# A Mamba-2 scan that is gated and normed in token rows, turned through DRAM

## The chip, the cores and the metric

The kernel runs on one core of a Trainium2 chip. The metric is the device time of one execution in microseconds (us), as a median over several runs.

## The reference

The kernel computes one layer of a hybrid decoder trunk over 256 tokens with 2048 features, all in float32: a token mixer with two branches (HGRN2 and Mamba-2), cross-attention into 256 memory tokens, a gated convolutional FFN, and norms between them. The change touches the Mamba-2 branch and the order around it. Cut to that:

```python
def mamba2_branch(z, xbc_raw, dt_raw, conv_w, conv_b, dt_bias, a_log, d_skip, norm_g):
    xbc = jax.nn.silu(causal_dwconv(xbc_raw, conv_w, conv_b))
    xs, bm, cm = jnp.split(xbc, [D_M2, D_M2 + M2_GROUPS * M2_DSTATE], axis=-1)
    dt = jax.nn.softplus(dt_raw + dt_bias)
    a_neg = -jnp.exp(a_log)
    y = ssd_chunk_scan(xs * dt[..., None], dt * a_neg, bm, cm)   # 8 groups of 4 heads of 64
    y = y + d_skip[:, :, None] * xs
    y = y.reshape(bsz, s, D_M2) * jax.nn.silu(z)
    yg = y.reshape(bsz, s, M2_GROUPS, D_M2 // M2_GROUPS)         # 256 features in a group
    yg = yg * lax.rsqrt(jnp.mean(yg * yg, axis=-1, keepdims=True) + M2_NORM_EPS)
    return yg.reshape(bsz, s, D_M2) * norm_g

def token_mixer(u, ...):
    hq, hf, hi, hog, mz, mxbc, mdt, g_hg, g_m2 = jnp.split(u @ w_in, idx, axis=-1)
    y_hg = hgrn2_branch(hq, hf, hi, hog, lb, hg_norm_g) @ w_branch_hg
    y_m2 = mamba2_branch(mz, mxbc, mdt, ...) @ w_branch_m2
    return (jax.nn.sigmoid(g_hg) * y_hg + jax.nn.sigmoid(g_m2) * y_m2) @ w_out
```

Group g of the Mamba-2 branch owns 256 features (two chunks of 128) of x, z and y, and 128 each of B and C. The gate and the norm work within a group, so a token's norm needs a sum over 256 features.

## The kernel before

**Matmuls.** Every weight is float32 and is cut into a high and a low part (ScalarE casts `hi`, L133; VectorE subtracts `lo`, L134), and a product is summed from three parts. Weights come in blocks of 1 MB; the list `order` fixes in which sequence SP loads them. `weights()` hands out the next block. I call the use of one block a step. There are two forms. `project` makes 128 features as rows and 256 tokens as columns ("channel rows"): 16 matmuls over 512 columns and 16 over 256 per block. `project_tok` takes four blocks and makes 2 x 128 tokens as rows and 512 features as columns ("token rows"): 24 matmuls over 512 columns per block. `raw` has 3 buffers, `hi` and `lo` have 5 halves of a block each, so casts run ahead of TensorE by up to about two blocks.

**Background.** A head's or a group's scan is a generator in the list `background`. At the start of every step each generator runs on to its next `yield`; `pause(n)` yields n times. TensorE's matmuls inside a step are pinned to that place. The other engines' instructions are put in order by a planner at build time, with its own costs; each engine then runs its queue in order, and an instruction that waits holds up what is behind it.

**The heads.** The 16 HGRN2 heads end with a turn between token rows and channel rows: `turned(y)` transposes 32x32 squares on VectorE (L503), writes the result to a DRAM tile by four transfers from POOL (L506), and reads it back in another order by one (L509). After `pause(gap)` `split_turned` scales it and cuts it into `hi` and `lo` (L515, L281, L282). `gap` is 4 steps, and 2 for the last head.

**Between.** `m2_dt` makes the steps dt and their running sums, and the Sigmoid of the first two HGRN2 gates stands at L796. The planner may put it earlier, since its input is there before the last heads.

**Mamba-2.** `m2_project(g)` makes six chunks of group g in channel rows: two of x, one of B, one of C (each with the convolution, L707 and L710) and two of z. `m2_scan(g)` then:

- takes Silu of all six chunks (L719) and builds the decays (L724 to L729); two steps later it multiplies C and B on TensorE, and turns the four 128x128 squares of x on TensorE (L747) to multiply by dt in token rows (L750);
- one step later makes the scan's product `yp` on TensorE, adds the D skip (L764), multiplies by Silu of z (L766), squares (L768) and adds the two chunks (L769);
- two steps later sums over the features by a matmul with `ones`, takes the inverse root of 128x256 values (L285, L286), and scales and cuts the result (L778, L281, L282).

`ym` holds the result for `project_tok(ym)`, the Mamba-2 branch's product. `gate()` makes the Sigmoid of 512 columns of a gate; the first two gates of this branch (`NF = 2`) come ahead of the first product, the others between the products. ScalarE holds one table of functions at a time; a function outside it takes an ACT_TABLE_LOAD.

Of the kernel before, what the change touches and what calls it, by code (L numbers as in the profile page):

```python
# [19 lines left out]
P = 128  # L20
# [44 lines left out]
def hybrid_trunk(ctx, tc, xT, memT, par, cst, msk, w_k0, w_ka, w_va, w_hg, w_hv, w_hog, w_ghg, w_bhg, w_dt,  # L65
                 w_m2, w_gm2, w_bm2, w_out, w_q, w_o, w_up, w_dn, fin_g, outT):
# [431 lines left out]
    def turned(y):  # L498

        yq = mp.tile([P, T], F32, name="yq", bufs=1)
        V.transpose(out=yq, in_=y)  # L503
        yd = dp.tile([P, T], F32, name="y_d", bufs=4)
        for b in range(P // B):
            G.dma_start(out=yd.rearrange("(n i) (b f) -> b i n f", i=B, b=P // B)[b],  # L506
                        in_=yq[b * B:(b + 1) * B, :].rearrange("i (n f) -> i n f", n=P // B))
        yc = mp.tile([P, T], F32, name="yc", bufs=2)
        G.dma_start(out=yc, in_=yd)  # L509
        return yc  # L510
# [8 lines left out]
    def hg_scan(h, kq, zz, v, sg):  # L519
# [102 lines left out]
        gap = 4 if h + 1 < HEADS else 2  # L622
        yield from pause(gap)
# [15 lines left out]
        yc = turned(y)  # L639
        yield from pause(gap)  # L640
# [17 lines left out]
    dt_tok = cp.tile([P, 2, 32], F32, name="dt_tok")  # L658
    cum_tok = cp.tile([P, 2, 32], F32, name="cum_tok")

    def m2_dt():
        ps = project(s2)
        rows = mp.tile([P, 2, T], F32, name="bb", bufs=1)
        raw, cum = rows[:, 0, :], rows[:, 1, :]
        join(mp, ps, raw)
        V.tensor_scalar(out=raw[0:32], in0=raw[0:32], scalar1=pc("dtb")[0:32], scalar2=None,
                        op0=ALU.add)
        w = mp.tile([P, T], F32, name="lf", bufs=1)
        softplus_neg_abs(raw[0:32], w[0:32])
        V.scalar_tensor_tensor(out=raw[0:32], in0=raw[0:32], scalar=0.0, in1=w[0:32],  # L670
                               op0=ALU.max, op1=ALU.add)
# [24 lines left out]

    def m2_project(g):
        sz = mp.tile([P, 6, T], F32, name="sz", bufs=2)
# [14 lines left out]
        for i in range(4, 6):  # L713
            ps = project(s2)
            join(mp, ps, sz[:, i, :])
        return sz, cb

    def m2_scan(g, sz, cb):
        S.activation(out=sz, in_=sz, func=AF.Silu)  # L719
# [24 lines left out]
        tp = pl.tile([P, 512], F32, name="lev")  # L744
        for q in range(2):
            for i in range(2):
                PE.transpose(tp[:, q * T + i * P:q * T + (i + 1) * P],  # L747
                             sz[:, i, q * P:(q + 1) * P], eye)
        xd = mp.tile([P, 2, T], F32, name="bb", bufs=1)
        V.tensor_tensor(out=xd.rearrange("p q (h c) -> p q h c", c=64),  # L750
                        in0=tp.rearrange("p (q h c) -> p q h c", q=2, c=64),
                        in1=free(dt_tok, 4 * g, [(32, 2), (1, 4), (0, 64)]), op=ALU.mult)
# [16 lines left out]
        V.tensor_tensor(out=sq[:, 0, :], in0=sq[:, 0, :], in1=sq[:, 1, :], op=ALU.add)  # L769
        yield True  # L770
        if g + 1 < GROUPS:
            yield True
        ps = pm_.tile([P, 512], F32, name="misc")
        mm(ps[:, 0:T], lhsT=ones, rhs=sq[:, 0, :], start=True, stop=True)
        r = mp.tile([P, T], F32, name="r", bufs=1)
        rsqrt(r, ps[:, 0:T], 1.0 / T, eps2_t)
        for i in range(2):
            V.scalar_tensor_tensor(out=y[:, i, :], in0=y[:, i, :], scalar=pc("m2_g", 2 * g + i),  # L778
                                   in1=r, op0=ALU.mult, op1=ALU.mult)
# [11 lines left out]
    scan = m2_scan(0, *m2_project(0))  # L791
    for c in range(4):
        o = pm[:, :, c * 512:(c + 1) * 512]
        if c < 2:
            sg = o
            S.activation(out=o, in_=o, func=AF.Sigmoid)  # L796
# [28 lines left out]
    sgs = [gate() for c in range(NF)]  # L825
    for c in range(4):
# [11 lines left out]
        if c + NF < 4:  # L838
            sgs.append(gate())
# [324 lines left out]
def _layout(inp):  # L1164
# [4 lines left out]
    z = _cols(cut(8192, 2048)).reshape(GROUPS, 2, P, 2048)  # L1169
# [20 lines left out]
    def put(name, a):  # L1190
# [35 lines left out]
        "w_m2": np.concatenate([xs, b, c, z], 1), "w_gm2": _toks(cut(16416, 2048)),  # L1226
# [24 lines left out]
```

## Time and profile before

| | |
|---|---|
| time, median of 3 runs | 2252.67 us (2252.03 to 2252.95) |
| the profiled execution | 2252.47 us, span 2250.7 us |
| TensorE busy | 2237.6 us, 99% of the span |
| VectorE busy | 1622.9 us, 72% |
| ScalarE busy | 1379.3 us, 61% |
| DMA | 441.11 MB, mean 196 GB/s |
| the heads, roughly | 160 to 560 us |
| the Mamba-2 groups 1 to 7, roughly | 700 to 980 us |

The busy share is read together with the chain of work that ended last, which says whose time set the end. A busy engine off that chain costs nothing by itself. All times on the page are from one execution.

### The profile page before, as it was taken

To read this page: it belongs to the slowest core of one execution; us is meant where nothing else is said; L and a number is where in the kernel's file an instruction comes from. 1 tells how busy PE (TensorE), PEld (TensorE's weight loads), DVE (VectorE), ACT (ScalarE), POOL (GpSimd) and SP (SyncE) were. 2 spreads that over 40 slices of the span, in tenths; PEclk is the share of its full clock that TensorE was granted. 3 is DMA by queue.
4 is the path that set the end of the run, shared out by engine and by line. 5 is a ranking of instruction groups with operands and counts; after the bars stand their busy time and mean duration, and the time that the engine had idled before them with its cause. 6 is when DMAs were issued, how large, how long until landed. Compare 5 with 4: busy or idle time off the path is not lost.

```text
span 2250.7 us, 33574 instructions
## 1 busy us (share of the span) xinstructions
PE 2237.6 (99%) x13188; PEld 1927.1 (86%) x13188; DVE 1622.9 (72%) x2602; ACT 1379.3 (61%) x2123; POOL 45.3 (2%) x89
## 2 busy tenths in 40 slices
PE   9999999999999999999999999999999999999998
PEld 8888888888888888888888888888888888888887
DVE  8858878887546677754566765677777777779787
ACT  7567677788546778764456655556555555555554
POOL 0000101101000000000000000000000000000000
PEclk9999999999999999999999999999999999999999
DMA  8655555555655555455566544476555555555554
GB/s 314 239 179 184 186 192 180 182 179 180 219 197 186 180 187 195 169 187 187 190 236 215 202 169 171 176 225 212 196 193 192 188 187 188 189 203 207 208 213 159
DMA packets 89502, 441.11 MB, mean 196 GB/s; under 512 B 25824, under 2 KB 30464, under 8 KB 40320
## 3 DMA queue, kind: packets, MB, share of 16 engines
q1 hardware_dynamic: 69600, 432.36, 54.2%
q0 software_dynamic: 2816, 4.20, 0.7%
q10 hardware_dynamic: 16928, 2.42, 0.6%
q8 instruction: 103, 1.69, 0.3%
q14 instruction: 55, 0.45, 0.1%
HBM read 430.52 MB, written 10.52 MB: 196 GB/s over the span
## 4 chain that ended last, share of the span: by engine, by line
PE 95%; ACT 2%; DVE 1%; DMA 1%; issue 1%; SPq 0%; POOL 0%; DVEq 0%; POOLq 0%; ACTq 0%
PE proj L82 86%; PE misc L82 5%; PE lev L82 4%; DVE lo L134 1%; ACT hi L133 0%; DMA yc<-y_d 0%; DMA raw<-in_w_k 0%; ACT L286 0%; DMA y_d<-yq 0%; DVE e L551 0%; ACT L285 0%; PE lev L747 0%; PE lev L816 0%; ACT y L638 0%; ACT misc L635 0%
## 5 line engine op out<-in xcount | busy, mean ns | idle before, releaser
L134 DVE TENSOR_TENSOR lo<-raw,hi 128x1024 fp32r<-128x1024 f32 x738 | 893.1, 1222 | 446.7 <-ACT hi L133 398.5
L133 ACT CAST hi<-raw 128x1024 fp32r<-128x1024 f32 x737 | 770.4, 1049 | 420.8 <-PE proj L82 391.1
L82 PE MATMUL proj<-s,hi 128*128 128x512 f32 x3696 | 873.4, 391 | 0.6 <-ACT hi L364 0.3
L82 PEld LDWEIGHTS proj<-s,hi 128*128 128x128 f32 x3696 | 685.2, 188 | 138.3 <-ACT hi L364 1.1
L82 PE MATMUL proj<-hi,s 128*128 128x512 f32 x1962 | 615.0, 390 | 0.0
L82 PEld LDWEIGHTS proj<-s,lo 128*128 128x128 f32 x3696 | 463.9, 192 | 14.2 <-DVE lo L134 2.1
L82 PE MATMUL proj<-s,lo 128*128 128x256 f32 x3696 | 472.2, 283 | 1.9 <-DVE lo L134 1.9
L82 PEld LDWEIGHTS proj<-hi,s 128*128 128x128 f32 x1962 | 368.1, 188 | 76.5 <-issue 0.3
L82 PE MATMUL proj<-lo,s 128*128 128x512 f32 x981 | 382.1, 390 | 1.0 <-DVE lo L134 1.0
L82 PEld LDWEIGHTS proj<-lo,s 128*128 128x128 f32 x981 | 184.2, 188 | 39.0 <-DVE lo L134 1.8
L266 ACT COPY jt<-proj 128x256 f32<-128x256 f32 x183 | 67.7, 370 | 99.6 <-PE proj L82 99.4
L168 ACT CAST hi<-raw 128x1024 fp32r<-128x1024 f32 (+1 forms) x56 | 52.2, 944 | 56.7 <-DVE raw L177 29.8
L169 DVE TENSOR_TENSOR lo<-raw,hi 128x1024 fp32r<-128x1024 f32 (+1 forms) x56 | 60.4, 1086 | 5.8 <-ACT hi L168 5.1
L710 DVE SCALAR_TENSOR_TENSOR sz<-t,par_t,sz 128x255 f32<-128x255 f32 (+2 forms) x96 | 46.1, 480 | 7.0 <-ACT sz L707 5.5
L983 DVE SCALAR_TENSOR_TENSOR gc<-g,par_t,gc 128x255 f32<-128x255 f32 x88 | 42.2, 480 | 2.0 <-ACT gc L981 0.6
L506 POOL DMA_DIRECT2D y_d<-yq x64 | 34.9, 552 | 378.1 <-DVE sm L610 266.8
L986 ACT ACTIVATE gc<-gc 128x256 f32<-128x256 f32 x44 | 18.4, 417 | 30.0 <-DVE gc L983 30.0
L82 PE MATMUL proj<-hi,ha 128*128 128x512 f32 x104 | 36.7, 389 | 0.0
L551 DVE TENSOR_TENSOR e<-bb 128x256 f32<-128x256 f32 x96 | 34.9, 417 | 0.1
L564 DVE TENSOR_TENSOR e<-e,kq 128x256 f32<-128x256 f32 x96 | 34.8, 415 | 0.0
L987 DVE TENSOR_TENSOR gc<-gc,r_f 128x256 f32<-128x256 f32 x44 | 18.7, 425 | 21.2 <-ACT gc L986 21.2
L555 ACT ACTIVATE e<-e 128x768 f32<-128x768 f32 x32 | 27.1, 846 | 10.6 <-DVE e L551 10.0
(301 smaller groups left out, 1761.5 us busy)
## 6 DMA issues: line engine op xcount, KB each, us to landing
raw<-in_w_up SPq DMA_DIRECT2D x88, 1024.0 KB, 4.8
raw<-in_w_m SPq DMA_DIRECT2D x48, 1024.0 KB, 4.8
raw<-in_w_dn SPq DMA_DIRECT2D x44, 1024.0 KB, 4.7
raw<-in_w_hg SPq DMA_DIRECT2D x32, 1024.0 KB, 4.8
raw<-in_w_hv SPq DMA_DIRECT2D x16, 1024.0 KB, 5.0
raw<-in_w_hog SPq DMA_DIRECT2D x16, 1024.0 KB, 4.8
raw<-in_w_ghg SPq DMA_DIRECT2D x16, 1024.0 KB, 4.8
raw<-in_w_bhg SPq DMA_DIRECT2D x16, 1024.0 KB, 4.8
```

The lines of the kernel that those rows point to most:

```text
L82: ins = PE.matmul(*args, **kwargs)
L133: S.copy(out=hi[:, c - a:d - a], in_=raw[:, c:d])
L134: V.tensor_tensor(out=lo[:, c - a:d - a], in0=raw[:, c:d], in1=hi[:, c - a:d - a].bitcast(F32), op=ALU.subtract)
L168: S.copy(out=hi[:, 0:d - c], in_=raw[:, c:d])
L169: V.tensor_tensor(out=lo[:, 0:d - c], in0=raw[:, c:d], in1=hi[:, 0:d - c].bitcast(F32), op=ALU.subtract)
L266: S.copy(out=tmp, in_=ps[:, T:2 * T])
L506: G.dma_start(out=yd.rearrange("(n i) (b f) -> b i n f", i=B, b=P // B)[b], in_=yq[b * B:(b + 1) * B, :].rearrange("i (n f) -> i n f", n=P ...
L551: V.tensor_tensor(out=lev[hw].rearrange("p (n c i) -> p n c i", c=2, i=hw), in0=free(bb, 0, [(2 * hw, nb), (T + hw, 2), (1, hw)]), in1=fre ...
L555: S.activation(out=e[j], in_=e[j], func=AF.Exp)
L564: V.tensor_tensor(out=ev, in0=ev, in1=free(kq, 0, [(2 * hw, nb), (T + hw, 2), (1, hw)]), op=ALU.mult)
L710: V.scalar_tensor_tensor(out=o[:, s:T], in0=raw[:, 0:T - s], scalar=pc("m2_cw", 4 * c + 3 - s), in1=o[:, s:T], op0=ALU.mult, op1=ALU.add)
L983: V.scalar_tensor_tensor(out=gc[:, s:T], in0=g[:, 0:T - s], scalar=pc("f_cw", 3 * c + 2 - s), in1=gc[:, s:T], op0=ALU.mult, op1=ALU.add)
```

## The change

z is no longer made in channel rows group by group, but in token rows, 512 columns for two groups at a time (`m2_gates`, with the weights' columns put in another order on the way in). x, after its Silu, goes to token rows by VectorE's 32x32 transpose and through DRAM, instead of by TensorE; the scan's y goes to token rows in the same way, is gated and normed there (squares of two tiles of 128 tokens, each with a sum along the row; no `ones` matmul), and goes back to channel rows in the same way. `turned` now takes a width and hands back the DRAM tile; the read stands at the caller. Between a write and the use of what is read there are 3, 3 and 4 steps (`pause`). Scans start a few steps later than before, according to the group. `m2_dt` writes each dt twice. The Exp of the scan is tied to a table that also has Ln. Three gates of the Mamba-2 branch stand behind the groups (`NF = 3`). The last head has a gap of 4 steps, and the Sigmoid at L796 is pinned to its place in ScalarE's order.

```diff
-    order += [w_dt[0]] + [w_m2[0, i] for i in range(6)]
+    order += [w_dt[0]] + [w_z[0, i] for i in range(4)] + [w_m2[0, i] for i in range(4)]
...
     for g in range(1, GROUPS):
-        order += [w_m2[g, i] for i in range(6)]
-    NF = 2
+        order += [w_z[g // 2, i] for i in range(4) if g % 2 == 0] + [w_m2[g, i] for i in range(4)]
+    NF = 3
...
-    def turned(y):
+    def turned(y, n, name):
-        yq = mp.tile([P, T], F32, name="yq", bufs=1)
+        yq = mp.tile([P, 64 * n], F32, name="yq", bufs=2)
         V.transpose(out=yq, in_=y)
-        yd = dp.tile([P, T], F32, name="y_d", bufs=4)
+        yd = dp.tile([n * B, T], F32, name=name, bufs=4)
         for b in range(P // B):
             G.dma_start(out=yd.rearrange("(n i) (b f) -> b i n f", i=B, b=P // B)[b],
-                        in_=yq[b * B:(b + 1) * B, :].rearrange("i (n f) -> i n f", n=P // B))
-        yc = mp.tile([P, T], F32, name="yc", bufs=2)
-        G.dma_start(out=yc, in_=yd)
-        return yc
+                        in_=yq[b * B:(b + 1) * B, :].rearrange("i (n f) -> i n f", n=n))
+        return yd
...
-        gap = 4 if h + 1 < HEADS else 2
-        yield from pause(gap)
+        yield from pause(4)
...
+    def m2_gates():
+        zt = mp.tile([P, 2, 512], F32, name="sg", bufs=2)
+        for q, ps in enumerate(project_tok(s2)):
+            S.copy(out=zt[:, q, :], in_=ps)
+        return zt
...
-        for i in range(4, 6):
-            ps = project(s2)
-            join(mp, ps, sz[:, i, :])
         return sz, cb
-    def m2_scan(g, sz, cb):
-        S.activation(out=sz, in_=sz, func=AF.Silu)
+    def m2_scan(g, sz, cb, zt):
+        yield from pause(0 if g in (0, GROUPS - 2, GROUPS - 1) else 1 + 2 * (g % 2))
+        xc = mp.tile([P, 2 * T], F32, name="w", bufs=1)
+        xv = xc.rearrange("p (m i t) -> p i m t", i=2, t=B)
+        S.activation(out=xv, in_=sz[:, 0:2, :].rearrange("p i (m t) -> p i m t", t=B), func=AF.Silu)
+        S.activation(out=sz[:, 2:4, :], in_=sz[:, 2:4, :], func=AF.Silu)
+        if g % 2 == 0:
+            S.activation(out=zt, in_=zt, func=AF.Silu)
+        yd = turned(xc, T // B, "x_d")
+        x = mp.tile([P, 2, T], F32, name="kq", bufs=2)
+        G.dma_start(out=x, in_=yd.rearrange("(q p) c -> p q c", p=P))
...
-        for j in range(2):
-            S.activation(out=lm[j], in_=lm[j], func=AF.Exp, scale=-1.0)
-        yield True
-        yield True
+        with tc.tile_critical():
+            nc.scalar.preload_act_table_set("natural_log_exp_and_others")
+            S.activation(out=lm[0], in_=lm[0], func=AF.Exp, scale=-1.0)
+        S.activation(out=lm[1], in_=lm[1], func=AF.Exp, scale=-1.0)
+        yield from pause(3)
...
-        tp = pl.tile([P, 512], F32, name="lev")
-        for q in range(2):
-            for i in range(2):
-                PE.transpose(tp[:, q * T + i * P:q * T + (i + 1) * P],
-                             sz[:, i, q * P:(q + 1) * P], eye)
         xd = mp.tile([P, 2, T], F32, name="bb", bufs=1)
-        V.tensor_tensor(out=xd.rearrange("p q (h c) -> p q h c", c=64), ...)
+        for q in range(2):
+            V.tensor_tensor(out=xd[:, q, :].rearrange("p (i b c) -> p i b c", i=2, c=B), in0=x[:, q, :]..., ...)
         yield True
...
-        V.tensor_tensor(out=y, in0=y, in1=sz[:, 4:6, :], op=ALU.mult)
-        sq = mp.tile([P, 2, T], F32, name="bb", bufs=1)
-        S.activation(out=sq, in_=y, func=AF.Square)
-        V.tensor_tensor(out=sq[:, 0, :], in0=sq[:, 0, :], in1=sq[:, 1, :], op=ALU.add)
-        yield True
-        if g + 1 < GROUPS:
-            yield True
-        ps = pm_.tile([P, 512], F32, name="misc")
-        mm(ps[:, 0:T], lhsT=ones, rhs=sq[:, 0, :], start=True, stop=True)
-        r = mp.tile([P, T], F32, name="r", bufs=1)
-        rsqrt(r, ps[:, 0:T], 1.0 / T, eps2_t)
+        yd = turned(y, T // B, "x_d")
+        yt = mp.tile([P, 2, T], F32, name="bb", bufs=1)
+        G.dma_start(out=yt, in_=yd.rearrange("(q p) c -> p q c", p=P))
+        yield from pause(3)
+        y = mp.tile([P, 2 * T], F32, name="kq", bufs=2)
+        r = mp.tile([P, 4], F32, name="rt", bufs=2)
+        for q in range(2):
+            V.tensor_tensor(out=y..., in0=yt[:, q, :]..., in1=zt[:, q, z0:z0 + T]..., op=ALU.mult)
+            S.activation(out=yt[:, q, :]..., in_=yv[:, q], func=AF.Square, accum_out=r[:, q:q + 1])
+        rsqrt(r[:, 2:4], r[:, 0:2], 1.0 / T, eps2_t)
+        for q in range(2):
+            S.activation(out=yv[:, q], in_=yv[:, q], func=AF.Copy, scale=r[:, 2 + q:3 + q])
+        yd = turned(y, T // B, "x_d")
+        yc = mp.tile([P, 2, T], F32, name="yc", bufs=2)
+        G.dma_start(out=yc, in_=yd.rearrange("(i p) t -> p i t", p=P))
+        yield from pause(4 if g + 1 < GROUPS else 3)
         for i in range(2):
-            V.scalar_tensor_tensor(out=y[:, i, :], in0=y[:, i, :], scalar=pc("m2_g", 2 * g + i), ...)
-            split(ym[:, 2 * g + i, :], y[:, i, :])
+            split_turned(ym[:, 2 * g + i, :], yc[:, i, :], pc("m2_g", 2 * g + i))
...
-            S.activation(out=o, in_=o, func=AF.Sigmoid)
+            tc.keep_in_program_order(S.activation(out=o, in_=o, func=AF.Sigmoid))
...
     for g in range(1, GROUPS):
-        background.append(m2_scan(g, *m2_project(g)))
+        if g % 2 == 0:
+            zt = m2_gates()
+        background.append(m2_scan(g, *m2_project(g), zt))
```

More of the change, by code (lines that the diff above doesn't have):

```diff
@@ L638, in hg_scan @@
             S.activation(out=yv[:, g], in_=yv[:, g], func=AF.Copy, scale=r[:, 2 + g:3 + g])
-        yc = turned(y)
-        yield from pause(gap)
+        yd = turned(y, P // B, "y_d")
+        yc = mp.tile([P, T], F32, name="yc", bufs=2)
+        G.dma_start(out=yc, in_=yd)
+        yield from pause(4)
         split_turned(yh[:, h, :], yc, pc("hg_g", h))
@@ L675, in m2_dt @@
                         op0=ALU.mult, op1=ALU.mult)
-        one = mp.tile([P, T], F32, name="r", bufs=1)
+        one = mp.tile([P, T], F32, name="jt", bufs=2)
         V.memset(one[0:32], 1.0)
@@ L690, in m2_dt_rows @@
                 tc.keep_in_program_order(ins)
-        V.tensor_copy(out=dt_tok, in_=ps[:, 0:64].rearrange("p (g h) -> p g h", g=2))
+        V.tensor_copy(out=dt_tok, in_=free(ps, 0, [(32, 2), (1, 32), (0, 2)]))
         V.tensor_copy(out=cum_tok, in_=ps[:, 64:128].rearrange("p (g h) -> p g h", g=2))
@@ L743, in m2_scan @@
                             op=ALU.mult)
-        tp = pl.tile([P, 512], F32, name="lev")
+        xd = mp.tile([P, 2, T], F32, name="bb", bufs=1)
         for q in range(2):
-            for i in range(2):
-                PE.transpose(tp[:, q * T + i * P:q * T + (i + 1) * P],
-                             sz[:, i, q * P:(q + 1) * P], eye)
[L749 to L752, printed above, removed]
+            V.tensor_tensor(out=xd[:, q, :].rearrange("p (i b c) -> p i b c", i=2, c=B),
+                            in0=x[:, q, :].rearrange("p (b i c) -> p i b c", i=2, c=B),
+                            in1=free(dt_tok, 64 * q + 8 * g, [(4, 2), (1, 4), (0, B)]), op=ALU.mult)
         yield True
@@ L761, in m2_scan @@
                       rhs=lm[j // 2][:, j % 2, T:3 * P], start=False, stop=True)
-        y = mp.tile([P, 2, T], F32, name="kq", bufs=2)
+        y = mp.tile([P, 2 * T], F32, name="kq", bufs=2)
+        yv = y.rearrange("p (m i t) -> p i m t", i=2, t=B)
         for i in range(2):
-            V.scalar_tensor_tensor(out=y[:, i, :], in0=sz[:, i, :], scalar=pc("m2_d", 2 * g + i),
-                                   in1=yp[:, i * T:(i + 1) * T], op0=ALU.mult, op1=ALU.add)
-        V.tensor_tensor(out=y, in0=y, in1=sz[:, 4:6, :], op=ALU.mult)
@@ L767, in m2_scan @@
-        sq = mp.tile([P, 2, T], F32, name="bb", bufs=1)
-        S.activation(out=sq, in_=y, func=AF.Square)
-        V.tensor_tensor(out=sq[:, 0, :], in0=sq[:, 0, :], in1=sq[:, 1, :], op=ALU.add)
-        yield True
-        if g + 1 < GROUPS:
-            yield True
-        ps = pm_.tile([P, 512], F32, name="misc")
-        mm(ps[:, 0:T], lhsT=ones, rhs=sq[:, 0, :], start=True, stop=True)
-        r = mp.tile([P, T], F32, name="r", bufs=1)
-        rsqrt(r, ps[:, 0:T], 1.0 / T, eps2_t)
+            V.scalar_tensor_tensor(out=yv[:, i], in0=xv[:, i], scalar=pc("m2_d", 2 * g + i),
+                                   in1=yp[:, i * T:(i + 1) * T].rearrange("p (m t) -> p m t", t=B),
+                                   op0=ALU.mult, op1=ALU.add)
@@ new lines, in m2_scan @@
+        yd = turned(y, T // B, "x_d")
+        yt = mp.tile([P, 2, T], F32, name="bb", bufs=1)
+        G.dma_start(out=yt, in_=yd.rearrange("(q p) c -> p q c", p=P))
+        yield from pause(3)
+        y = mp.tile([P, 2 * T], F32, name="kq", bufs=2)
+        r = mp.tile([P, 4], F32, name="rt", bufs=2)
+        z0 = g % 2 * T
+        yv = y.rearrange("p (n q c) -> p q n c", q=2, c=B)
+        for q in range(2):
+            V.tensor_tensor(
+                out=y.rearrange("p (i b q c) -> p q b i c", i=2, q=2, c=B)[:, q],
+                in0=yt[:, q, :].rearrange("p (b i c) -> p b i c", i=2, c=B),
+                in1=zt[:, q, z0:z0 + T].rearrange("p (b i c) -> p b i c", i=2, c=B), op=ALU.mult)
+            S.activation(out=yt[:, q, :].rearrange("p (n c) -> p n c", c=B), in_=yv[:, q],
+                         func=AF.Square, accum_out=r[:, q:q + 1])
@@ L790, in hybrid_trunk @@
     m2_dt()
-    scan = m2_scan(0, *m2_project(0))
+    zt = m2_gates()
+    scan = m2_scan(0, *m2_project(0), zt)
     for c in range(4):
@@ L823, in turn_later @@
         turn(c)
-    sgs = [gate() for c in range(NF)]
+    sgs = [gate("sg" if c == 2 else "sz") for c in range(NF)]
     for c in range(4):
@@ L838, in hybrid_trunk @@
         if c + NF < 4:
-            sgs.append(gate())
+            sgs.append(gate("sg"))
     drain()
@@ L1168, in _layout @@
     hg = np.stack([_cols(cut(0, 2048)), _cols(cut(2048, 2048))], 1)
-    z = _cols(cut(8192, 2048)).reshape(GROUPS, 2, P, 2048)
+    swap = np.arange(D).reshape(GROUPS, 2, P // B, B).transpose(0, 2, 1, 3).ravel()
     xs = _cols(cut(10240, 2048)).reshape(GROUPS, 2, P, 2048)
```

15 lines of the change are left out of this document (7 added, 8 removed).

## The prediction

> **What bounds the kernel now.** First the page: the share of busy time and the chain that ended last.
>
> ```profile
> PE 2237.6 (99%) x13188; PEld 1927.1 (86%) x13188; DVE 1622.9 (72%) x2602; ACT 1379.3 (61%) x2123; POOL 45.3 (2%) x89
> PE 95%; ACT 2%; DVE 1%; DMA 1%; issue 1%; SPq 0%; POOL 0%; DVEq 0%; POOLq 0%; ACTq 0%
> ```
>
> TensorE is never idle for long, and 95% of the chain is its own instructions. A change pays here in two ways only: TensorE gets less work, or one of its few holes closes. It costs by opening a new hole. So I priced TensorE's work in the Mamba-2 stage from the chain in order of time (start, length, what), and within one group from TensorE's timeline.
>
> ```profile
> 714.14 38.93 PE proj L82 x224
> 754.16 5.56 PE proj L82 x32
> 759.72 1.50 PE misc L82 x16
> 761.22 11.35 PE proj L82 x64
> 773.00 16.70 PE proj L82 x96
> 790.79 5.56 PE proj L82 x32
> 986.84 119.73 PE proj L82 x528
> ```
>
> ```profile
> 772.40 0.59 PE L82 MATMUL misc<-bb,ones 128*128 128x256 f32 x2
> 772.65 4.03 PE L82 MATMUL proj<-s,hi 128*128 128x512 f32 x16
> 789.54 0.82 PE L82 MATMUL misc<-sz 128*128 128x256 f32 x4
> 790.19 0.60 PE L747 MATMUL lev<-cst_t,sz 128*128 128x128 f32 x4
> 790.55 1.67 PE L82 MATMUL proj<-s,lo 128*128 128x256 f32 x12
> ```
>
> One group of the steady state lasts 36.63 us (754.16 to 790.79). I call the use of one 1 MB weight block a step. A step of `project` has 32 matmuls and took 38.93 / 7 = 5.561 us; a step of `project_tok` has 24 and took 119.73 / 22 = 5.442 us. Six steps are 33.4 us; the other 3.3 us are the scan's own matmuls.
>
> Then the holes: the waits of TensorE between 440 and 1010 us (total, times, longest), its timeline around the end of the heads, where the brackets give idle time and its releaser, and what ScalarE and VectorE did there.
>
> ```profile
> PE proj L82 <- DVE lo L134: 2.9, 3, 1.9
> ```
>
> ```profile
> 561.94 1.88 PE L82 MATMUL proj<-s,lo 128*128 128x256 f32 x8 [1.93 <-DVE lo L134]
> 563.62 8.35 PE L82 MATMUL proj<-s,hi 128*128 128x512 f32 x32
> 577.36 0.50 PE L82 MATMUL proj<-lo,s 128*128 128x512 f32 x1 [0.51 <-DVE lo L134]
> 780.34 7.44 PE L82 MATMUL proj<-s,hi 128*128 128x512 f32 x32
> ```
>
> ```profile
> 531.88 1.28 ACT L796 ACT_TABLE_LOAD   x1
> 557.31 1.28 ACT L286 ACT_TABLE_LOAD   x1
> 559.72 0.45 DVE L503 STREAM_TRANSPOSE yq<-y 128x256 f32<-128x256 f32 x1 [4.15 <-ACT y L638]
> 574.14 0.51 ACT L515 ACTIVATE jt<-yc,par_t 128x256 f32<-128x256 f32 x1 [5.45 <-DMA yc<-y_d]
> ```
>
> From the last heads to the first m2 branch products TensorE stands three times, 2.9 us: 1.93 and 0.51 here, and 0.45 earlier. The Mamba-2 stage has no hole. Behind the middle one, 32 matmuls took 8.35 us where the same 32 take 7.44, 0.9 more. The first big hole comes from the last head's squares: a Sigmoid of L796 has been put between the last heads (531.88), so Ln and Exp load a table each (the Exp's is shown), VectorE stands 4.15 us before the transpose, and the weights' subtractions are queued behind it. The other is the last head's trip through DRAM: with a gap of two steps ScalarE waits 5.45 us, and TensorE loses 0.51. The two waits also calibrate the buffers: 4 to 5.5 us of a blocked queue cost TensorE 0.5 to 1.9 us.
>
> **The change part by part.**
>
> *z in token rows.* Sixteen `project` steps become sixteen `project_tok` steps: 16 x (5.561 - 5.442) = 1.9 us off TensorE, directly on the path. The number of weight blocks and of SP's transfers is unchanged.
>
> *The `ones` matmul goes.* The chain has 772.57 to 773.00 for it, 0.43 us with the slower matmul behind it. Eight groups: 3.4 us.
>
> *The four transposes on TensorE go.* 790.19 to 790.55, 0.36 us. Eight groups: 2.9 us. The sum off TensorE is 8.2 us.
>
> *The heads' end.* The pinned Sigmoid no longer comes between the last heads' Ln and Exp, so those loads go; ScalarE gets them back, and VectorE's 4.15 us wait shrinks. The last head's gap of four steps covers a trip that took two steps and 5.45 us. And behind `m2_dt` there now come four `project_tok` steps whose results need two copies only, where `m2_project` had joins and convolutions. I take all 2.9 us; bounds 0 (another late wait takes the place) and 3.8 (with the 0.9 of the slow restart). Late next is the weights' own cast, which then waits for TensorE as it does elsewhere.
>
> *Three trips through DRAM per group.* The nearest row is the heads' trip, here head 8: its matmuls, POOL's four writes, POOL's read back, the first use on ScalarE; then the landings over all heads.
>
> ```profile
> 386.25 0.83 PE L82 MATMUL misc<-vc,a 128*128 128x128 f32 x6
> ...
> 391.93 2.18 POOL L506 DMA_DIRECT2D y_d<-yq  x4 [19.91 <-DVE sm L610]
> 395.94 0.57 POOL L509 DMA_DIRECT2D yc<-y_d  x1 [1.83 <-ACT hi L133]
> ...
> 406.70 0.51 ACT L515 ACTIVATE jt<-yc,par_t 128x256 f32<-128x256 f32 x1
> ```
>
> ```profile
> raw<-in_w_m SPq DMA_DIRECT2D x48, 1024.0 KB, 4.8
> y_d<-yq POOLq DMA_DIRECT2D x64, 32.0 KB, 1.8
> yc<-y_d POOLq DMA_DIRECT2D x16, 128.0 KB, 4.7
> cum_d<-bb SPq DMA_DIRECT2D x1, 32.0 KB, 1.5
> xr<-in_xT SPq DMA_DIRECT2D x8, 256.0 KB, 5.0
> ...
> DMA to landing us min/median/max: 2.4/4.7/6.5
> ...
> DMA to landing us min/median/max: 1.8/1.8/6.5
> ```
>
> With four steps the first use stands 406.70 - 386.25 = 20.5 us behind the matmuls, and the data was there after 395.94 + 4.7 - 386.25 = 14.4 us: 6.1 us to spare. With three steps (5.5 us less) the use would come at about 15 us. The new y trip (yp, D skip, transpose, write, read) carries 256 KB each way. Against the head's: +0.7 us for yp (1.50 to 0.83), +0.45 for a transpose twice as wide, +0.3 for the read (5.0 to 4.7), about -2 because the squares and the scaling are not in it. That is some 14 us: it just arrives. With the longest landings instead of the medians (+4.7 and +1.8) it takes 20.5 us and VectorE waits 5.5 us. Behind that wait stand the weights' subtractions, and TensorE waits for those. x starts on ScalarE, ahead of TensorE, has the same three steps and one more until yp: it has more room. The third trip has four steps. Each trip is five transfers on POOL, which waits for the write before it issues the read, so trips run one behind the other: 2.18 + 1.8 + 0.57 = 4.6 us each, three per 36 us; its queue is not full, but x of the next group and the normed rows of this one are a step apart. What VectorE waits is covered if the buffers are full, and the group's row says that it has room:
>
> ```profile
> 754.16:790.79 36.63, 36.63 (x220) 32.01 (x220) 27.50 (x43) 29.09 (x43) 0.00 (x0) 1.00 0.54 187
> L503 DVE STREAM_TRANSPOSE yq<-y 128x256 f32<-128x256 f32 x16 | 7.1, 443 | 11.6 <-ACT y L638 11.5
> L778 DVE SCALAR_TENSOR_TENSOR kq<-kq,par_t,r 128x256 f32<-128x256 f32 x2 | 0.9, 480 | 2.3 <-ACT r L286 2.3
> L769 DVE TENSOR_TENSOR bb<-bb 128x256 f32<-128x256 f32 x1 | 0.4, 418 | 0.0
> L267 DVE TENSOR_TENSOR sz<-proj,jt 128x256 f32<-128x256 f32 x2 | 0.8, 416 | 0.0
> ```
>
> VectorE is busy 27.50 us of 36.63 and loses 0.9 + 0.4 + 0.8 = 2.1 (norm, sum of squares, z joins). It gains three transposes of 128x512, 0.45 to 0.89 each, 1.3 to 2.7: the same load, with 9 us of room. ScalarE (29.09) gets seven copies, squares and scalings of 128x256 at 0.4 to 0.5 us, some 3 us, and sheds two of four table loads at 1.28 each and the wide Ln and Exp: no net load. I take 1.5 us of new TensorE holes over the stage; bounds 0 and 8 x (1.93 + 0.9) = 22.6 us, nearer the lower, since the median trip arrives. Below nothing it can't go, as TensorE has no hole there now.
>
> *DRAM traffic.* 24 trips of 512 KB are 12.6 MB in about 290 us, 43 GB/s on top of 187, at a DMA share of 0.54; a weight block lands in 4.8 us of a 5.5 us step, with three buffers. Costed at nothing; without that cover it would be part of the late-trip rival.
>
> A rule weighed against rows: 32 KB written through POOL in pieces of 256 bytes landed in 1.8 us, 32 KB on SP in long rows in 1.5. The Trainium skill ("DMA: Bandwidth & Descriptors", Specifications) says that below 512 bytes a piece costs a read-modify-write; by the rows that is at most 0.3 us here. The same page (Anatomy of one DMA — SWDGE (gpsimd) path) fits 2.0 us + bytes / 436 GB/s: an estimate of 2.6 us for the 256 KB read where the nearest rows have 4.7 and 5.0; by it the trip ends 2 us sooner and the sum loses its 1.5.
>
> *Three branch gates.* The same steps in another order; the last group's scan gets twelve steps of cover for eleven. Free; with one trip late there is still the order of the sixteen chunks before it is missed.
>
> *Sum.* Profiled execution 2252.47 us (its span 2250.7; the median of the runs is 2252.67, 0.2 more): 2252.47 - 8.2 - 2.9 + 1.5 = 2242.9; with half of the slow restart, 2242.5.
>
> **The rivals.**
>
> *Late trips (slower).* The place is VectorE's product of yt and z, three steps behind yp. For it: the last heads' landings came near the maxima, and the new transfers have twice the bytes. Against: a median trip is in time and VectorE has 9 us of room. Price: 1.93 + 0.9 per group, 22.6 us: 2252.5 - 12 + 22.6 = 2263. It decides from 1.5 us of lost TensorE time per group. What would make trips late, as a mechanism of this kernel, is POOL's issue held up beside VectorE: each of five issues late by one VectorE instruction (0.89 us for the wide transpose) makes 4.5 us a trip, about the same lateness. The nearest row, where 64 issues ran beside VectorE's transposes and copies, speaks against:
>
> ```profile
> L506 POOL DMA_DIRECT2D y_d<-yq x64: 548/550/680, 196.3 to 562.1; - x64
> ```
>
> The Trainium skill ("SBUF — State Buffer", SBUF: two separate sides) warns of just this: VectorE in a two-port mode keeps GpSimd from writing descriptors, and the transfer seems to stall. By the row, hardly ever here.
>
> *Partly late (no change).* About 1.0 us per group, 8 us: 2252.5 - 12 + 8 = 2248.5, and up to 2252. For and against as above.
>
> *The heads' end stays (faster, by less).* The planner lets another function's table in between the last heads, or the holes move to another place there: 2252.47 - 8.2 = 2244.3, to 2246 with the 1.5.
>
> **How the numbers follow.** Forecast 0.60, heads' end stays 0.16, partly late 0.13, late 0.11. A change under 0.2% (4.5 us) can't be told from none. Faster 0.76, same 0.13, slower 0.11. Range: from 2239 (12 us off and a little more, if the fp32 matmuls' neighbours gain too) to 2251, which leaves out most of the late case and the top of the partly late one.
>
> **What would show it.** Groups in pairs of about 71.2 us (twice 36.63, less 2 x (0.43 + 0.36) and 4 x 0.119); no idle TensorE between 520 and 600 us; no table loads in the last four heads; VectorE's waits for yt and x under 3 us. Wrong: idle TensorE once or twice per group, released by a VectorE subtraction, with a wait on a read-back in front of it.

## The result: 0.5% slower, and the profile after

The changed kernel takes 2263.1 us (2262.89 to 2267.76) where the kernel before, run beside it, takes 2252.49 (2252.03 to 2252.95): a ratio of 1.005, 95% interval 1.0038 to 1.0063. The forecast was 2242.5. The profiled execution took 2263.27 us, its span 2261.1.

From the page of the changed kernel, the busy times and the chain that ended last:

```profile
PE 2233.0 (99%) x13012; PEld 1916.3 (85%) x13012; DVE 1622.3 (72%) x2602; ACT 1388.9 (61%) x2181; POOL 118.1 (5%) x209
PE 56%; ACT 1%; DVE 1%; issue 0%; ACTq 0%; DVEq 0%
```

TensorE has 176 instructions fewer, and is busy 4.6 us less; the span is 10.4 us longer. So some 15 us are new idle time. The chain, 95% TensorE before, can be followed back for little more than half of the span here, so I read the stretches instead. Busy time by stretch shows where (after start and end: length, then TensorE, its weight loads, VectorE, ScalarE and POOL with their counts, then TensorE's granted clock, DMA share, GB/s); first the changed kernel, then the kernel before.

```profile
520.00:560.00 40.00, 40.00 (x286) 33.74 (x286) 24.40 (x47) 25.83 (x46) 2.73 (x5) 1.00 0.61 211
560.00:600.00 40.00, 40.00 (x202) 34.09 (x201) 27.12 (x38) 31.15 (x44) 5.77 (x10) 1.00 0.66 231
700.00:800.00 100.00, 100.00 (x544) 85.75 (x543) 69.03 (x98) 67.27 (x103) 15.22 (x25) 1.00 0.64 214
800.00:1010.00 210.00, 192.94 (x1005) 160.99 (x1004) 142.30 (x215) 168.69 (x270) 50.90 (x84) 0.98 0.61 205
```

```profile
800.00:1010.00 210.00, 210.00 (x1187) 181.29 (x1186) 147.60 (x216) 160.35 (x228) 0.00 (x0) 1.00 0.52 181
```

The holes at the heads' end are gone, and 210 - 192.94 = 17.1 us of new ones stand between 800 and 1010 us, in the later groups. TensorE's waits from 440 to 1010 us say who released them (total, times, longest):

```profile
PE proj L82 <- DVE lo L134: 9.9, 4, 3.7
PE misc L82 <- DVE e L758: 3.4, 7, 1.2
PE misc L82 <- DVE bb L762: 2.4, 1, 2.4
```

ScalarE's cast makes one more wait, of 1.1 us. A VectorE subtraction leads, as the late rival said. But the rival's cause, a wait on a read-back in front of it, is next to nothing: in 700 to 1010 us VectorE waits 0.4 us in all for the x that is read back and never for y, and ScalarE 2.1 us, in two places, for the rows that come back by the third trip (the longer one, 1.85 us, ends 13 us ahead of the matmul at 911.62). Here is the hole at 868 us, in the timelines of ScalarE, VectorE and TensorE:

```profile
861.70 1.28 ACT L746 ACT_TABLE_LOAD   x1
862.99 0.85 ACT L746 ACTIVATE e<-e 128x768 f32<-128x768 f32 x1
866.61 1.28 ACT L744 ACT_TABLE_LOAD   x1 [2.77 <-PE proj L82]
867.90 0.84 ACT L745 ACTIVATE e<-e 128x768 f32<-128x768 f32 x1
868.65 1.03 ACT L133 CAST hi<-raw 128x1024 fp32r<-128x1024 f32 x1
869.71 1.23 DVE L134 TENSOR_TENSOR lo<-raw,hi 128x1024 fp32r<-128x1024 f32 x1 [7.13 <-ACT hi L133]
858.03 7.44 PE L82 MATMUL proj<-s,hi 128*128 128x512 f32 x32
870.99 1.22 PE L82 MATMUL proj<-s,lo 128*128 128x256 f32 x8 [2.65 <-DVE lo L134]
872.05 9.05 PE L82 MATMUL proj<-s,hi 128*128 128x512 f32 x32
```

Read it from the end. TensorE stands 2.65 us until VectorE's `lo`; VectorE stood 7.13 us until ScalarE's cast; ScalarE's cast is queued behind the Exp in the section; and ScalarE stood still, with nothing to compute, from 863.8 to 866.6 in front of the section's table. The second Exp (L746) doesn't depend on the section, has overtaken it at 862.99, and has paid a table load of its own. Behind the hole the same 32 matmuls take 9.05 us, where those ahead of it took 7.44. The other three waits for a subtraction end at 911.62, 951.12 and 982.64 us, each 5 to 8 us behind a section's load (906.29, 944.18 and 974.87).

Before the loads of all eight sections ScalarE waited 18.1 us. What ended these waits (releaser: us, times):

```profile
  PE proj L82: 8.4, 2
  DMA raw<-in_w_m: 2.4, 1
  DMA vc<-cum_d: 2.3, 1
  DMA x_d<-yq: 1.6, 1
  DMA raw<-in_w_gm: 1.5, 1
  DMA raw<-in_w_z: 1.0, 1
  ACT e L740: 1.0, 1
```

Only the last of these makes the Exp's input. The others are projections, weight blocks of later steps, running sums for the next group and the trip of x: work that was planned ahead of the section, on whichever engine or queue. So ScalarE doesn't enter `tc.tile_critical()` before all of that is done. The rows show it for TensorE, for weight blocks and running sums that SP loads, and for POOL's trips; whether the entry waits for every engine and every queue, they don't show. ScalarE, which runs ahead of TensorE by the blocks in `hi` and `lo`, has to let TensorE catch up, eight times. What it has left of its lead shows in its waits for TensorE to give a half block of `hi` free, 700 to 1010 us, in the kernel before and then in the changed one:

```profile
ACT hi L133 <- PE proj L82: 35.5, 22, 2.5
```

```profile
ACT hi L133 <- PE proj L82: 20.3, 13, 2.1
```

An engine that waits for a buffer to come free is as far ahead as it can be. That happened 22 times before and 13 times after.

### The profile page after: what moved, and what is told of

Its sections match the earlier page's. It is cut to its first block, busy times and chain, and to the rows that moved or that the text cites. A ratio compares the mean times of both kernels' runs of the same rounds, so it can differ in the third digit from the quotient of the medians.

```text
span 2261.1 us, 33653 instructions
## 1 busy us (share of the span) xinstructions
PE 2233.0 (99%) x13012; PEld 1916.3 (85%) x13012; DVE 1622.3 (72%) x2602; ACT 1388.9 (61%) x2181; POOL 118.1 (5%) x209
## 4 chain that ended last, share of the span: by engine, by line
PE 56%; ACT 1%; DVE 1%; issue 0%; ACTq 0%; DVEq 0%
PE proj L82 49%; PE misc L82 4%; PE lev L82 3%; DVE lo L134 0%; ACT hi L133 0%; PE lev L844 0%; DVE e L758 0%; ACT L285 0%; ACTq L743 0%; PE lev L924 0%; ACT bb L794 0%; ACT L727 0%; ACT L286 0%; ACT L728 0%; ACT sz L728 0%
## 5 line engine op out<-in xcount | busy, mean ns | idle before, releaser
L82 PE MATMUL proj<-s,hi 128*128 128x512 f32 x3440 | 810.7, 391 | 1.4 <-ACT hi L364 1.4
L82 PEld LDWEIGHTS proj<-s,hi 128*128 128x128 f32 x3440 | 638.0, 188 | 129.1 <-ACT hi L364 1.9
L82 PE MATMUL proj<-hi,s 128*128 128x512 f32 x2218 | 695.7, 390 | 1.1 <-ACT hi L133 1.1
L82 PEld LDWEIGHTS proj<-hi,s 128*128 128x128 f32 x2218 | 416.3, 188 | 88.3 <-ACT hi L133 1.7
L82 PEld LDWEIGHTS proj<-s,lo 128*128 128x128 f32 x3440 | 433.3, 192 | 21.4 <-DVE lo L134 5.8
L82 PE MATMUL proj<-s,lo 128*128 128x256 f32 x3440 | 441.1, 284 | 9.2 <-DVE lo L134 9.2
L82 PE MATMUL proj<-lo,s 128*128 128x512 f32 x1109 | 431.8, 389 | 0.8 <-DVE lo L134 0.8
L82 PEld LDWEIGHTS proj<-lo,s 128*128 128x128 f32 x1109 | 208.4, 188 | 43.2 <-DVE lo L134 1.1
L266 ACT COPY jt<-proj 128x256 f32<-128x256 f32 x167 | 61.7, 370 | 84.8 <-PE proj L82 84.7
L505 POOL DMA_DIRECT2D x_d<-yq x96 | 55.8, 587 | 314.6 <-DVE yq L502 311.5
L717 DVE SCALAR_TENSOR_TENSOR sz<-t,par_t,sz 128x255 f32<-128x255 f32 (+2 forms) x96 | 45.6, 475 | 17.1 <-ACT sz L714 16.1
```

The lines of the kernel that those rows point to most:

```text
L82: ins = PE.matmul(*args, **kwargs)
L266: S.copy(out=tmp, in_=ps[:, T:2 * T])
L717: V.scalar_tensor_tensor(out=o[:, s:T], in0=raw[:, 0:T - s], scalar=pc("m2_cw", 4 * c + 3 - s), in1=o[:, s:T], op0=ALU.mult, op1=ALU.add)
```

## The experiments

Four theories: the *section* (it waits for work that it doesn't need; theory A in the texts below); the *named table* in it; *late trips* (B, the rival whose number, 2263, came out); and ScalarE's *load*, its table loads above all (C).

**e1, no section and no named table.**

```diff
-        with tc.tile_critical():
-            nc.scalar.preload_act_table_set("natural_log_exp_and_others")
-            S.activation(out=lm[0], in_=lm[0], func=AF.Exp, scale=-1.0)
-        S.activation(out=lm[1], in_=lm[1], func=AF.Exp, scale=-1.0)
+        for j in range(2):
+            S.activation(out=lm[j], in_=lm[j], func=AF.Exp, scale=-1.0)
```

> The changed kernel with the two Exp of the scan as they were before: no critical section and no named table. Theory A (the critical section makes ScalarE wait until everything that was put in order ahead of it is done on every engine and DMA queue, once per group, and the casts of the weights behind it come late): TensorE's 17 us of holes between 800 and 1000 us go, and the time is what the prediction's sum had, 2241 to 2245 us. Rival B (a trip through DRAM comes late once per group and blocks VectorE or ScalarE): the trips are untouched, the time stays at 2260 to 2264 us. Rival C (ScalarE's table loads, which are more in number now): it gets no fewer loads here, so 2258 to 2264 us.

2247.1 us against 2252.93, ratio 0.9972 (0.9961 to 0.9984). The slowdown is gone, with all trips left as they are. TensorE's idle time between 800 and 1010 us falls from 17.1 to 5.4 us:

```profile
800.00:1010.00 210.00, 204.59 (x1080) 171.29 (x1079) 149.14 (x224) 180.40 (x287) 51.61 (x85) 1.00 0.66 223
```

Ahead of the largest of these holes VectorE waits for the scaled rows of the norm, whose Ln and Exp have loaded a table each:

```profile
945.32 1.28 ACT L285 ACT_TABLE_LOAD   x1
947.19 1.28 ACT L286 ACT_TABLE_LOAD   x1
950.47 0.71 DVE L502 STREAM_TRANSPOSE yq<-kq 128x512 f32<-128x512 f32 x1 [2.98 <-ACT kq L796]
955.33 0.88 PE L82 MATMUL misc<-e,bb 128*64 128x256 f32 x8 [2.37 <-DVE e L756]
```

The holes of 1.23 us at 938.65 and of 0.53 at 970.16 stand behind three and four loads in a row: there the planner has put Silu and Exp in turns, and the weights' casts come after them.

**e2, the section with its named table, put into the kernel before.**

```diff
-        for j in range(2):
-            S.activation(out=lm[j], in_=lm[j], func=AF.Exp, scale=-1.0)
+        with tc.tile_critical():
+            nc.scalar.preload_act_table_set("natural_log_exp_and_others")
+            S.activation(out=lm[0], in_=lm[0], func=AF.Exp, scale=-1.0)
+        S.activation(out=lm[1], in_=lm[1], func=AF.Exp, scale=-1.0)
```

> The kernel before with the critical section and the named table around the first Exp of the scan, and nothing else of the change. Theory A: ScalarE stands 1 to 6 us ahead of it in each of eight groups; 2255 to 2275 us, holes of TensorE in the Mamba-2 stage where there were none. B: no trip through DRAM exists in that stage, 2252 us, no change. C: fewer table loads, 2250 to 2252 us.

2257.65 us, ratio 1.002 (1.001 to 1.0029): 4.7 us for the section, with no Mamba-2 trip in the kernel. Its loads, the first of them, TensorE's hole behind that, and the stretch, here and (last row) in the kernel before:

```profile
L729 ACT ACT_TABLE_LOAD x8 | 10.3, 1283 | 14.1 <-PE proj L82 8.2 <-DMA raw<-in_w_m 2.5 <-DVE bb L771 2.2
575.82 1.28 ACT L729 ACT_TABLE_LOAD   x1 [8.24 <-PE proj L82]
578.95 0.50 PE L82 MATMUL proj<-hi,s 128*128 128x512 f32 x1 [3.14 <-DVE t L267]
560.00:700.00 140.00, 134.59 (x595) 111.04 (x594) 70.71 (x70) 67.67 (x79) 2.74 (x5) 0.98 0.55 194
560.00:700.00 140.00, 137.57 (x614) 114.23 (x614) 75.08 (x76) 67.36 (x77) 2.74 (x5) 0.99 0.57 201
```

ScalarE waits again, 14.1 us over eight sections. Only the first, 8.24 us, gets through to TensorE: it is idle 140 - 134.59 = 5.4 us in that stretch, 3.0 more than in the kernel before. The other 5.9 us are covered, and between 700 and 1010 us TensorE has no wait. So the section costs what the buffers can't cover. This run isn't the section alone: in the order of the kernel before, the named table also does for Ln and Exp, and ScalarE's loads between 700 and 1010 us fall from 32 to 17, its busy time from 232.49 to 216.66 us. That the section is covered there for this reason is likely, not shown.

**e3, the named table without a section.** In place of the section:

```diff
+        tc.keep_in_program_order(
+            nc.scalar.preload_act_table_set("natural_log_exp_and_others"))
+        tc.keep_in_program_order(
+            S.activation(out=lm[0], in_=lm[0], func=AF.Exp, scale=-1.0))
```

> The changed kernel with the named table and the first Exp pinned in ScalarE's program order, without a critical section. Theory A: no wait on other engines is left, 2241 to 2246 us, near the plain Exp. B: 2260 to 2264 us. C: near the changed kernel if its loads stay as many.

2247.66 us, ratio 0.9975 (0.9966 to 0.9985): as e1. The two pins keep their own order, but they don't keep other work out from between: the named load at 858.39 us is followed by a Silu's load at 861.02 and then by another for the Exp itself, at 863.46. It is so in two of the seven groups behind 700 us.

**e5, the section without the named table:**

```diff
         with tc.tile_critical():
-            nc.scalar.preload_act_table_set("natural_log_exp_and_others")
             S.activation(out=lm[0], in_=lm[0], func=AF.Exp, scale=-1.0)
```

> The changed kernel with the critical section around the first Exp, but without the named table in it. It tells the section's wait from the table. Theory A (the section waits for every engine and queue): 2258 to 2264 us, as slow as the changed kernel. If the named table were what costs: 2245 to 2249 us, as the plain Exp.

2260.09 us, ratio 1.003 (1.0018 to 1.0042). The section without the table keeps 13 of the 16 us (2260.09 against e1's 2247.1), and the named table without a section costs nothing (e3). The last 3 us come only with both; no run explains them.

**e4, the section kept, the trips longer:** in all groups y gets four steps out and the back trip three; in groups 1 to 5 x gets four as well and starts a step earlier.

```diff
-        yield from pause(0 if g in (0, GROUPS - 2, GROUPS - 1) else 1 + 2 * (g % 2))
+        early = 0 < g < GROUPS - 2
+        yield from pause(2 * (g % 2) if early else 0)
...
-        yield from pause(3)
+        yield from pause(4 if early else 3)
...
-        yield from pause(3)
+        yield from pause(4)
...
-        yield from pause(4 if g + 1 < GROUPS else 3)
+        yield from pause(3)
```

> The changed kernel with four steps instead of three for y's trip (three for the last one), and for x's trip in groups 1 to 5, which start a step earlier. The critical section stays. Theory A: 2258 to 2266 us, the waits ahead of the critical section stay. B: a trip has 5.5 us more, so the holes close and it is 2241 to 2250 us.

2261.88 us, ratio 1.0038 (1.0023 to 1.0052): 1.2 us between medians for a step more of room, and the intervals overlap. TensorE's time in the groups is that of the changed kernel, and ScalarE waits 16.9 us before the section's loads:

```profile
800.00:1010.00 210.00, 193.89 (x1001) 161.61 (x1001) 142.03 (x215) 169.47 (x270) 49.01 (x81) 0.97 0.61 203
```

That falls against late trips.

**e6, the heads' end alone, in the kernel before:**

```diff
-        gap = 4 if h + 1 < HEADS else 2
+        gap = 4
...
-            S.activation(out=o, in_=o, func=AF.Sigmoid)
+            tc.keep_in_program_order(S.activation(out=o, in_=o, func=AF.Sigmoid))
```

> The kernel before with the heads' end alone: a gap of four steps for the last head and the pinned Sigmoid. The prediction's term: TensorE's three holes (2.9 us, with the slow restart 3.8) close, 2248.5 to 2250 us. If these holes only move to another place there: 2251 to 2253 us.

2248.28 us against 2253.3, ratio 0.9977 (0.9968 to 0.9986). Medians give 5.0 us, the spans 2250.7 - 2246.6 = 4.1. No wait of TensorE is left between 440 and 1130 us:

```profile
440.00:560.00 120.00, 120.00 (x981) 103.73 (x980) 99.62 (x219) 87.31 (x167) 13.72 (x25) 1.00 0.54 189
560.00:700.00 140.00, 140.00 (x642) 116.09 (x641) 72.28 (x73) 68.54 (x82) 2.75 (x5) 1.00 0.56 200
```

**e7, e1 with the scan of group 7 two steps later.** In e1 the four loads at 960 us stand where the last two groups' scans meet, so I spaced them:

```diff
-        yield from pause(0 if g in (0, GROUPS - 2, GROUPS - 1) else 1 + 2 * (g % 2))
+        yield from pause({0: 0, GROUPS - 2: 0, GROUPS - 1: 2}.get(g, 1 + 2 * (g % 2)))
```

> The plain Exp, and group 7's scan starts two steps later, so that it stands six steps behind group 6's as the other groups do, instead of four. Theory: what is left of the holes at 2247 us (1.2, 2.4 and 0.5 us around 940 to 970 us) comes from group 7 waiting for the tiles of group 6 (its decays are written into the same buffers, and ScalarE waits for yp): 2243 to 2245 us. Rival: ScalarE is simply too full there with table loads (six per group): 2246 to 2248 us.

2247.03 us, as e1: a miss. The spacing of the scans is not what is left. Nor is it the bare number of table loads: between 700 and 1010 us there are 37 here and 41 in e1, at the same time.

**e8, fewer table loads, no section.** e3's two lines, e7's start, the second Silu pinned behind the first, and a table with Ln and Exp named ahead of the norm's inverse root:

```diff
-        S.activation(out=sz[:, 2:4, :], in_=sz[:, 2:4, :], func=AF.Silu)
+        tc.keep_in_program_order(
+            S.activation(out=sz[:, 2:4, :], in_=sz[:, 2:4, :], func=AF.Silu))
...
-        rsqrt(r[:, 2:4], r[:, 0:2], 1.0 / T, eps2_t)
+        tc.keep_in_program_order(
+            nc.scalar.preload_act_table_set("natural_log_exp_and_others"))
+        tc.keep_in_program_order(
+            S.activation(out=r[:, 2:4], in_=r[:, 0:2], func=AF.Ln, bias=eps2_t, scale=1.0 / T))
+        S.activation(out=r[:, 2:4], in_=r[:, 2:4], func=AF.Exp, scale=-0.5)
```

> As the run with plain Exp and the later group 7, with the table that has both Ln and Exp named and pinned ahead of the scan's Exp and ahead of the norm's Ln, and the two Silu pinned together: some eight table loads fewer, no critical section. If table loads on ScalarE cost what is left: 2241 to 2243 us; if not: as the run without it, 2243 to 2247 us.

**2240.91 us** (2240.32 to 2241.3) against 2253.3, ratio 0.9943 (0.993 to 0.9957): faster than the kernel before and than e1. Between 700 and 1010 us there are 32 table loads; TensorE loses 0.1 us in the groups, and ScalarE has its lead again:

```profile
800.00:1010.00 210.00, 209.88 (x1106) 176.22 (x1105) 153.33 (x227) 175.31 (x287) 53.36 (x88) 1.00 0.68 228
ACT hi L133 <- PE proj L82: 41.4, 34, 3.7
```

**e9, e8 without e7's start** (e7's diff undone).

> The 2241 us version without the later start of group 7 (back to four steps behind group 6). If the later start has no part in its gain: 2240 to 2242 us. If the fewer table loads and the later start are needed together: 2243 to 2246 us, with holes around 940 to 970 us.

2240.41 us (2239.87 to 2243.73), ratio 0.9949 (0.9934 to 0.9963): the start plays no part here either.

**e10, e8 with the section put back, nothing else.**

```diff
-        tc.keep_in_program_order(
-            nc.scalar.preload_act_table_set("natural_log_exp_and_others"))
-        tc.keep_in_program_order(
-            S.activation(out=lm[0], in_=lm[0], func=AF.Exp, scale=-1.0))
+        with tc.tile_critical():
+            nc.scalar.preload_act_table_set("natural_log_exp_and_others")
+            S.activation(out=lm[0], in_=lm[0], func=AF.Exp, scale=-1.0)
```

> The 2241 us version with the critical section put back around the table and the first Exp, and nothing else: the disputed cost in a kernel without holes. Theory A: holes come back in the Mamba-2 stage; between 2245 us (what the section cost in the kernel before, 4.7 us) and 2257 us (what it cost in the changed kernel, 16 us). Rival B: 2241 us.

2257.15 us (2253.33 to 2259.24), ratio 1.0018 (1.0009 to 1.0028): 16 us between medians, with the section in place of two pins as the only difference from e8. ScalarE's waits at it, TensorE's time, and VectorE's waits for x:

```profile
L744 ACT ACT_TABLE_LOAD x8 | 10.3, 1283 | 18.2 <-DMA x_d<-yq 6.2 <-DMA raw<-in_w_gm 4.9 <-DMA vc<-cum_d 4.0
800.00:1010.00 210.00, 200.19 (x1050) 166.77 (x1049) 146.27 (x219) 166.09 (x271) 50.97 (x84) 0.98 0.64 216
DVE bb L762 <- DMA kq<-x_d: 11.4, 3, 5.3
```

The profiled execution (2253.35) is one of the shorter ones, so 9.8 us idle here is the lower end. Part of it goes by way of the trips: at the section of 967.28 us VectorE stands 6.5 us for ScalarE before it can start the transposes of y and x; then it waits 5.3 us for that x, and TensorE 2.2 us behind it. In e8 VectorE waits 7.6 us for x, never over 2.7. So here the section itself makes trips late. How much of the 16 us is its wait, and how much the other order that the planner builds around it (30 table loads here, 32 in e8), no run tells apart.

**e11, e8 with a shorter trip:** y gets two steps out, and the back trip one more.

```diff
-        yield from pause(3)
+        yield from pause(2)
...
-        yield from pause(4 if g + 1 < GROUPS else 3)
+        yield from pause(5 if g + 1 < GROUPS else 4)
```

> The 2241 us version with two steps instead of three for y's trip and one more for the last trip: rival B made true, so that its price is seen. The trip then lacks some 4 to 6 us in each group, and VectorE waits that long for yt: holes in every group, 2243 us (0.3 per group) to 2263 us (2.8 per group). If the buffers cover it all: 2241 us.

2246.05 us (2241.79 to 2251.43), ratio 0.9968 (0.9959 to 0.9978): some 5 us between medians. But the expected wait did not come. In the profiled execution (2242.98 us) VectorE never waits for y, so with two steps y's trip still arrives. TensorE has one hole, and in front of it stands a trip that is late, but the third one, for which ScalarE waits:

```profile
934.57 0.91 ACT L512 ACTIVATE jt<-yc,par_t 128x256 f32<-128x256 f32 x2 [3.28 <-DMA yc<-x_d]
940.99 1.85 PE L82 MATMUL misc<-e,bb 128*64 128x256 f32 x16 [3.12 <-DVE bb L761]
```

This is what a late trip looks like, once and for 3.1 us of TensorE's time. It doesn't give the price of eight, and where the longer executions, up to 2251.43 us, lost their time is not known.

**e12, e8 without the pin of the second Silu.**

```diff
-        tc.keep_in_program_order(
-            S.activation(out=sz[:, 2:4, :], in_=sz[:, 2:4, :], func=AF.Silu))
+        S.activation(out=sz[:, 2:4, :], in_=sz[:, 2:4, :], func=AF.Silu)
```

> The 2241 us version with the second Silu not pinned behind the first, so that an Exp can come between them and a table more is loaded. If the count of table loads on ScalarE is what costs: 2242 to 2245 us. If the named table at the norm does it alone: 2240 to 2242 us.

2242.81 us (2242.06 to 2244.54), ratio 0.9957 (0.9942 to 0.9972): 1.9 us above e8 between medians, though the two intervals overlap. The larger part of e8's gain over e1, 4.3 us, is there without this pin. It comes with the table that is named at the norm, since the one at the scan alone gains nothing (e3) and the later start nothing (e9).

Together the runs make a table of four: without the section 2240.9 (e8) and 2247.1 (e1), with it 2257.2 (e10) and 2263.1 (the changed kernel). The section costs 16 us in both rows, and what e8 adds is worth 6 us in both columns. That the section is the first is shown by e10, which changes nothing else, and by e1 and e5, which take it out and keep it without its table. That the second is table loads is argued from e8's edit and the rows of e1; by e7 their number alone doesn't decide, and which of them count was not tested one by one.

## Why the prediction was wrong, point by point

*The step that failed* is in the paragraph on the three trips: ScalarE "sheds two of four table loads at 1.28 each ... no net load", with 1.5 us of new holes. The section was read there as a table choice, and its own wait had no term at all. It costs 16 us (e10; e1 against the changed kernel). The 17.1 us of holes stand where the sum had 1.5. The trace of the kernel before had the row, and I did not look for it: the one section of that kernel, around a table and a cast in `weights` (L130), has ScalarE wait for a transfer that the cast doesn't read.

```profile
L130 ACT ACT_TABLE_LOAD x1 | 1.3, 1283 | 4.7 <-DMA hr<-rows_d 4.7
```

An estimate from that row: eight such waits are 38 us on ScalarE; by the prediction's own calibration (4 to 5.5 us of a blocked queue cost 0.5 to 1.9) that is 4 to 15 us of TensorE time, and the sum would have come to 2246 to 2258.

*The loads* went up and not down: 36 in 700 to 1010 us, 32 before. A named table serves only until the next Silu, which the planner may put between it and the Ln, and the unnamed Ln and Exp still load one each. The prediction's reading of the table was right for the order of the kernel before (17 loads in e2), not for the new order. ScalarE's busy time between 800 and 1010 us is 168.69 us of 210, before 160.35.

*The rival with the right number had the wrong mechanism.* Late trips gave 2263 and a VectorE subtraction as releaser; both came true. But e4 gives the trips a step more and gains 1.2 us, and e1 leaves them alone and gains 16. The test that the prediction named, "with a wait on a read-back in front of it", tells them apart: 0.4 us on VectorE and 2.1 on ScalarE are all that is there, none of it directly in front of one of the four subtractions. That the number came out is chance.

*What held.* Work off TensorE, 8.2 us: in e8 `yp` of every second group starts, by the chain in order of time, at

```profile
775.00 1.50 PE misc L82 x16
846.01 1.50 PE misc L82 x16
917.01 1.50 PE misc L82 x16
```

71.0 us a pair of groups, forecast 71.2. The sum without new holes, 2252.47 - 8.2 - 2.9 = 2241.4, is near e8's 2240.9; but e8 has pins and a named table that the forecast kernel lacks, so this bears out the terms and not the forecast.

The heads' end was worth 4.1 to 5.0 (e6), where 2.9 was taken, with a bound of 3.8 that e6's interval (3.2 to 7.2 us) takes in: mis-sized, in the safe direction. Between 440 and 560 us ScalarE loads one table, the first section's, where it loaded 15. The transposes of 128x512 took 0.70 us, between the bounds of 0.45 and 0.89.

The trips arrive: in e8, where TensorE is not held up, VectorE waits for x 7.6 us in four places and 2.7 at most, forecast under 3, for y 0.5 us, and it is covered. The forecast's reason for y, a trip of some 14 us that "just arrives" at 15, was too tight. The reads landed in 4.2 to 4.8 us (medians in e8), near the 5.0 taken, and the writes, of 64 KB each, in 3.7, where the heads' 1.8 was kept; but the first use stands 21 to 23 us behind `yp` in the three groups above, not 15, as here:

```profile
787.54 0.72 POOL L781 DMA_DIRECT2D bb<-x_d  x1 [3.50 <-ACT hi L133]
796.39 0.42 DVE L789 TENSOR_TENSOR kq<-bb,sg 128x256 f32<-128x256 f32 x1
```

So y still arrives with two steps (e11). POOL's issues beside VectorE's wide transposes, on the page of the changed kernel:

```profile
L505 POOL DMA_DIRECT2D x_d<-yq x96 | 55.8, 587 | 314.6 <-DVE yq L502 311.5
```

They took 587 ns each, where the narrow ones took 550. What the Trainium skill ("SBUF — State Buffer", SBUF: two separate sides) warns of, POOL held back from writing descriptors beside VectorE in a two-port mode, doesn't show in the length of an issue; whether these transposes run in such a mode, no run tells.

## What to carry to other kernels

Before pricing what a section, a pin or a fence *does*, price what it *waits for*: find one in the trace before, read the idle time in front of its first instruction and who released it, and ask whether the engine it stands on lives from running ahead. To fix a table's place, a pin of the load and its user to the engine's own order cost nothing here, where the section cost 16 us; but look in the trace whether other functions have come between the two (e3). And a rival that gives the right number isn't shown by it: its own wait must be in the trace.

## What the hardware showed that I had not expected

A hole of 2.65 us in TensorE was followed by a lower clock: 0.91 granted in the 20 us around it, and the 32 matmuls behind it took 1.6 us longer. A hole of 2.77 us, 40 us later in the same execution, was not: the granted clock stayed at 1.00, and the 32 matmuls behind it took 7.44 us.

```profile
860.00:880.00 20.00, 17.35 (x85) 14.67 (x84) 11.11 (x20) 16.16 (x25) 2.26 (x4) 0.91 0.57 205
900.00:920.00 20.00, 17.23 (x84) 14.40 (x84) 9.05 (x12) 17.32 (x28) 2.60 (x4) 1.00 0.62 220
911.62 1.22 PE L82 MATMUL proj<-s,lo 128*128 128x256 f32 x8 [2.77 <-DVE lo L134]
912.68 7.44 PE L82 MATMUL proj<-s,hi 128*128 128x512 f32 x32
```

The Trainium skill ("TensorE: Matmul & The Clock Gate", HAM oscillation) warns of idle gaps over about 3.4 us; here a shorter one was enough, and its length alone doesn't decide. In the changed kernel a hole can cost over half as much again as its length (1.6 us behind 2.65), or nothing more.

A table load took 1283 ns wherever it stood, with the next instruction right behind it (866.61 + 1.28 = 867.89, the Exp at 867.90). The Trainium skill ("ScalarE: Activation LUTs", What ACT_TABLE_LOAD costs) adds a drain of some 1.4 us to each; none stands between load and use here, nor in front of the load: in e1 an Exp ends at 962.98 + 0.84 = 963.82 and the next load starts at 963.83. ScalarE's queue has drains at the sections, of 2.03 us in the median. In e10 one runs from 967.42 us for 2.00, to 969.42, where the section's Exp ends too (968.57 + 0.85), and the second Exp starts at 969.52. So the drain runs beside the load and the Exp, and adds next to nothing to them; what ScalarE loses at a section is the wait in front of it.
